# A block with timeline scheduling around the whole of a two-layer hybrid backbone

## The chip, the cores and the metric

The kernel runs on one core of one Trainium2 chip. The metric is device microseconds (us) of one execution. The core has five engines that take their instructions from queues of their own, in order: TensorE (PE, with its weight loads shown as PEld), VectorE (DVE), ScalarE (ACT), GpSimd (POOL) and SyncE (SP, which here only issues DMAs). An instruction that waits for a semaphore holds up all that stands behind it in the same queue. What stands where in these queues is fixed when the program is built.

## The reference

Two layers work on 1024 latent tokens and 256 context tokens of width 1024, all in float32:

```
for l in range(DEPTH):                      # 2
    mod = silu(c) @ w_mod[l] + b_mod[l]     # shift, scale, gate; also for c_ctx
    h  = rmsnorm(x,  g_pre[l]) * (1 + scale)   + shift
    hc = rmsnorm(xc, g_pre[l]) * (1 + scale_c) + shift_c
    u, uc = even_mixer(...) if l == 0 else odd_mixer(...)
    x = x + gate * rmsnorm(u @ w_out[l], g_post[l])
    if l == 0: xc = xc + gate_c * rmsnorm(uc @ w_out[l], g_post[l])

# even_mixer, per head (8 of them), m = 0, 1 two score maps
p[m] = softmax(rope(q[m]) @ rope(k[m]).T / 8)       # 1024+256 keys, 256 for context queries
o = rmsnorm((p[0] - lam * p[1]) @ v) * 0.8 * silu(g)
# beside it a gated short convolution over 1024 channels: b * conv3(c * h) * silu(g)
# odd_mixer: 16 heads of 2-D neighbourhood attention (NA), and
# 4 heads of gated linear attention (GLA) scanned in both directions
```

## The kernel before

One Python class, `Kernel`, writes the program. The methods are called one after the other, and each engine operation that they issue goes to a scheduler, which forms the five queues: among the operations that are ready in its own model of the machine it takes the one with the best priority. The priority is the place in the program, moved at some lines by offsets. So the queues don't follow the text of the program; the scheduler's model of how long things take decides what is put between what.

The weights come in units of 512 KB. `load_w` (L225) issues the DMA on SP, and `split_w` cuts the weight into a high part `whi` (ACT, L242) and a low part `wlo` (POOL or DVE, L243). `proj_chunk` (L438) multiplies one unit with one chunk of the tokens: 24 matmuls (8 steps of the contraction, times hi by hi, hi by lo and lo by hi) into a PSUM tile `pj`, of which there are two. A chunk has 512, 512 or 256 tokens.

Layer 0 runs eight heads of differential attention (`diff_head`). For each, k and q are projected and pass through `rope`: ACT copies the `pj` tile into an SBUF tile `ropex` (L517), which frees the `pj` tile, and DVE and POOL turn it. A head then has ten score blocks, each for two maps: `S` matmuls (L590), the row maximum on DVE (L592), the exponential on ACT (L594), DVE's combination of the two maps (L600), transposes on PE (`atr`, L612), their copies (L615, L616) and the products with v (`av`, L626). There is one `S` tile, so the next `S` matmuls wait until ACT has read the last. The head ends in `norm`: three `ms` matmuls (L636), then `rstd` with a Ln (L308) and an Exp (L309) on ACT and three passes on DVE (L310 to L312), the product with the gate (L638) and the DMA to DRAM (L639). Two buffers matter here:

```
big = self.ap.tile([P, 1280], F32, name="ropex", tag="p0", bufs=2)                                # in rope
r = self.rstd(ap.tile([P, TOK], F32, name="rs", tag="p0", bufs=2), ...)                           # in norm
```

`ropex`, the first map's probabilities and the norm's `rs` take turns in the same two buffers, `p0`. While `rs` holds one, from L309 to L638, the ropes have the other alone. Between the blocks the program calls `ws.run(1 + qt)`, which issues projection chunks of the convolution (`c4.0` and so on) and of w_mod as work that does not depend on the softmax.

The output projection `out0` (L754) follows; its three-bank pool takes the PSUM place of `S` and `ms`. Layer 1 has the GLA heads (gates `gz`, levels L1120 to L1162, key transposes `gktr` L1213, states and outputs L1233 and L1245) and the NA heads (scores L1464, L1465, products L1490, transposes L1513), and the second output projection.

At the start the program loads x, the sixteen early w_mod units and a small set of rows `rowsB` (L166), which PE transposes (`trB`, L169).

Of the kernel before, what the change touches and what calls it, by code (L numbers as in the profile page):

```python
# [39 lines left out]
class Stream:  # L40
# [39 lines left out]
    def run(self, n):  # L80
        for _ in range(n):
            if not self.step():
                return
# [15 lines left out]
class Kernel:  # L99
# [6 lines left out]
        return (ctx or self.ctx).enter_context(self.tc.tile_pool(name=name, bufs=bufs, **kw))  # L106

    def run(self):
        self.setup()
        with ExitStack() as es:  # L110
            self.hp = self.pool("hp", ctx=es)
            rope_es, out_es = ExitStack(), ExitStack()
            self.start(rope_es)
            conv_es = self.layer0(rope_es)
            self.layer1(self.out0(conv_es, out_es), out_es)
            with ExitStack() as es2:
                self.out1(es2)
# [1523 lines left out]
```

## Time and profile before

| | |
|---|---|
| median of 3 runs | 3095.2 us (3093.76 to 3097.55) |
| profiled execution | 3095.5 us, of which the span of the trace is 3093.7 us |
| PE busy | 2942.9 us, 95% of the span |
| PE weight loads busy | 2452.9 us, 79% |
| DVE, ACT, POOL busy | 1879.2, 1530.6 and 965.5 us |

PE's busy time is that of its matmuls from start to modelled end, and these overlap; a group of eight matmuls shows 1.98 us and the next group starts 1.82 us after it. The time that the profile lays down as idle before an instruction is time in which the engine had nothing running.

### The profile page before, as it was taken

What the parts mean: (1) busy time and instruction counts of PE and PEld (TensorE: products, weight loads), DVE (VectorE), ACT (ScalarE), POOL (GpSimd) and SP (SyncE); (2) the same over time, 40 slices, a digit from 0 to 9 for tenths busy, and PEclk for the clock granted to TensorE, in tenths of its full rate; (3) what the DMA queues carried; (4) which work ended last, traced back from release to release, by engine and by line L of the source; (5) the groups of instructions that cost most, each with busy time, mean ns of one, the idle gap of its engine ahead of it and who ended that gap; (6) DMA issues with size and microseconds to landing.
All of it is one profiled execution on the core that took longest, in us unless ns stands there. A gap on an engine that the chain in (4) does not pass through costs nothing. (4 is left out here: it accounts for less than half of the span.)

```text
span 3093.7 us, 42416 instructions
## 1 busy us (share of the span) xinstructions
PE 2942.9 (95%) x16244; PEld 2452.9 (79%) x16244; DVE 1879.2 (61%) x3149; ACT 1530.6 (49%) x2853; POOL 965.5 (31%) x765
## 2 busy tenths in 40 slices
PE   6999999999999999999999998999999999999898
PEld 4888888888888887888877777778777888887686
DVE  5675757575665757564244767575736666667723
ACT  4553535353544445453344665665635555556522
POOL 3213130313021211205233232322235555556622
PEclk9999999999999999999999999999999999999999
DMA  6111111211110211115342112111131111112323
GB/s 227 35 45 48 49 46 33 65 35 58 35 58 28 65 35 48 45 42 207 111 149 74 45 35 72 50 48 58 55 95 31 47 49 44 43 44 98 118 75 123
DMA packets 236982, 206.46 MB, mean 67 GB/s; under 512 B 43591, under 2 KB 194538, under 8 KB 236778
## 3 DMA queue, kind: packets, MB, share of 16 engines
q1 hardware_dynamic: 236778, 203.74, 21.4%
q8 instruction: 128, 2.10, 0.3%
q14 instruction: 76, 0.62, 0.1%
HBM read 168.04 MB, written 35.67 MB: 66 GB/s over the span
## 5 line engine op out<-in xcount | busy, mean ns | idle before, releaser
L243 POOL TENSOR_TENSOR wlo<-wraw,whi 128x1024 fp32r<-128x1024 f32 x149 | 371.6, 2494 | 1164.5 <-ACT whi L242 1014.9
L438 PE MATMUL pj<-hBh,whi 128*128 128x512 f32 (+1 forms) x1712 | 382.0, 353 | 9.7 <-ACT hBh L354 4.8
L438 PE MATMUL pj<-hBl,whi 128*128 128x512 f32 (+1 forms) x1712 | 370.3, 350 | 0.9 <-DVE hBl L355 0.9
L438 PE MATMUL pj<-hBh,wlo 128*128 128x512 f32 (+1 forms) x1712 | 350.7, 345 | 0.0
L242 ACT CAST whi<-wraw 128x1024 fp32r<-128x1024 f32 x176 | 184.5, 1048 | 308.7 <-PE ops L754 188.3
L438 PEld LDWEIGHTS pj<-hBh,whi 128*128 128x128 f32 x1712 | 275.3, 191 | 45.2 <-ACT hBh L354 5.4
L438 PEld LDWEIGHTS pj<-hBh,wlo 128*128 128x128 f32 x1712 | 278.7, 191 | 37.2
L438 PEld LDWEIGHTS pj<-hBl,whi 128*128 128x128 f32 x1712 | 279.5, 193 | 35.7 <-DVE hBl L355 1.1
L438 PE MATMUL pj<-hAh,whi 128*128 128x512 f32 x968 | 279.5, 409 | 14.6 <-ACT ropex L517 13.0
L438 PE MATMUL pj<-hAh,wlo 128*128 128x512 f32 x968 | 255.3, 398 | 0.0
L438 PE MATMUL pj<-hAl,whi 128*128 128x512 f32 x968 | 254.6, 394 | 0.0
L592 DVE TENSOR_REDUCE st<-S 128x1 f32<-128x1280 f32 (+1 forms) x160 | 203.8, 1274 | 79.3 <-PE S L590 79.3
L594 ACT ACTIVATE p<-S,st 128x1280 f32<-128x1280 f32 (+1 forms) x160 | 186.1, 1163 | 82.1 <-DVE st L592 80.5
L1472 POOL TENSOR_TENSOR np<-np,nst 128x640 f32<-128x640 f32 x128 | 166.6, 1304 | 192.3 <-DVE nst L1471 154.4
L438 PEld LDWEIGHTS pj<-hAh,wlo 128*128 128x128 f32 x968 | 181.0, 189 | 36.1
L438 PEld LDWEIGHTS pj<-hAh,whi 128*128 128x128 f32 x968 | 170.2, 191 | 47.9 <-ACT ropex L517 14.4
L438 PEld LDWEIGHTS pj<-hAl,whi 128*128 128x128 f32 x968 | 178.1, 189 | 34.7
L590 PE MATMUL S<-kst,qd 128*128 128x512 f32 (+1 forms) x832 | 192.3, 361 | 0.2 <-ACT p L594 0.2
L590 PEld LDWEIGHTS S<-kst,qd 128*128 128x128 f32 x832 | 137.1, 188 | 40.2 <-ACT p L594 21.5
L1468 DVE CUSTOM_DVE_ANT_0 np<-NS,nB 128x640 f32<-128x640 f32 x128 | 105.3, 823 | 90.4 <-PE NS L1465 84.5
L615 ACT CAST ath<-atr 128x512 fp32r<-128x512 f32 (+1 forms) x208 | 99.2, 505 | 113.5 <-PE atr L612 112.9
L1523 DVE TENSOR_TENSOR ptl<-ntr,pth 128x512 fp32r<-128x512 f32 (+2 forms) x224 | 117.5, 536 | 49.6 <-ACT pth L1522 45.7
(361 smaller groups left out, 6219.3 us busy)
## 6 DMA issues: line engine op xcount, KB each, us to landing
wraw<-in_ev_w_in_dram SPq DMA_DIRECT2D x64, 512.0 KB, 4.1
wraw<-in_od_w_in_dram SPq DMA_DIRECT2D x56, 512.0 KB, 3.9
wraw<-in_w_out_dram SPq DMA_DIRECT2D x55, 512.0 KB, 3.8
wraw<-in_w_mod_dram SPq DMA_DIRECT2D x48, 512.0 KB, 3.8
sgT<-gt SPq DMA_DIRECT2D x32, 256.0 KB, 2.0
uT<-sg SPq DMA_DIRECT2D x8, 640.0 KB, 3.5
nG<-in_rpbp_dram SPq DMA_DIRECT2D x128, 40.0 KB, 2.3
xt<-in_x_dram SPq DMA_DIRECT2D x8, 512.0 KB, 5.9
```

Source lines behind the costliest of these rows:

```text
L242: nc.scalar.copy(out=hi, in_=u.raw)
L243: (nc.vector if u.lo_eng == "v" else nc.gpsimd).tensor_tensor(out=lo, in0=u.raw, in1=hi.bitcast(F32), op=ALU.subtract)
L438: nc.tensor.matmul(ps[:, 0:tn], lhsT=a[:, k, :], rhs=self.h_at(k, t0, tn)[b], start=n == 0, stop=n == 23)
L590: nc.tensor.matmul(S[:, c0:c0 + tn], lhsT=qd[:, 2 * m + part, P * qt:P * qt + P], rhs=self.kst[m][:, t0:t0 + tn], start=part == 0, stop=pa ...
L592: nc.vector.tensor_reduce(out=st[:, m:m + 1], in_=S[:, 0:n], axis=AX.X, op=ALU.max, negate=True)
L594: nc.scalar.activation(out=p[m][:, 0:n], in_=S[:, 0:n], func=AF.Exp, bias=st[:, m:m + 1], accum_out=st[:, 2 + m:3 + m])
L615: nc.scalar.copy(out=dh, in_=tv)
L1468: nc.vector.tensor_tensor_reduce(out=p, in0=S[:, z0:z0 + 640], in1=bias[2 * i + m][:, c0:c0 + 640], scale=1.0, scalar=3e38, op0=ALU.add, o ...
L1472: nc.gpsimd.tensor_tensor(out=p, in0=p, in1=st[:, 2:3].broadcast_to([P, 640]), op=ALU.mult)
L1523: nc.vector.tensor_tensor(out=lv[:, s:e], in0=tr[:, s:e], in1=hv[:, s:e].bitcast(F32), op=ALU.subtract)
```

## The change

All of the program is put into one block of the tile framework, with a flag that makes the scheduler use another model of the machine (its timeline model) to decide the order. The computation, the number of instructions on every engine and the tiles stay as they are. The lines behind the new method stand four further down: L438 becomes L442, L590 becomes L594, L636 becomes L640.

```diff
     def run(self):
+        with self.tc.block(schedule_with_timeline_sim=True):
+            self.work()
+
+    def work(self):
         self.setup()
         with ExitStack() as es:
             self.hp = self.pool("hp", ctx=es)
```

The order of every queue is another. First place: PE at the end of the first head, from the last `ms` matmul on (`pj` are projection matmuls; `hA` and `hB` are the tokens, h high and l low). Before:

```order
L636 MATMUL ms<-qf,onesD 128x256
L438 MATMUL pj<-hAh,wlo 128x512 x8
L289 MATMUL modtr<-sel,modrow 128x2 x2
L438 MATMUL pj<-hBh,whi 128x512 x8
L438 MATMUL pj<-hBl,whi 128x512 x8
L438 MATMUL pj<-hBh,wlo 128x512 x8
L438 MATMUL pj<-hBh,whi 128x256 x8
L438 MATMUL pj<-hBl,whi 128x256 x8
L438 MATMUL pj<-hBh,wlo 128x256 x8
```

Of the change, at the same place:

```order
L640 MATMUL ms<-qf,onesD 128x256
L442 MATMUL pj<-hBh,whi 128x256 x8
L442 MATMUL pj<-hBl,whi 128x256 x8
L442 MATMUL pj<-hBh,wlo 128x256 x8
L442 MATMUL pj<-hAh,whi 128x512 x8
L442 MATMUL pj<-hAl,whi 128x512 x8
L442 MATMUL pj<-hAh,wlo 128x512 x8
```

In before, what follows `ms` are chunks of the convolution and, behind the rows shown, two more groups of 24 matmuls of 512 columns, before the first chunk whose `pj` tile a rope copy of the next head has to free. In the change, the next head's first two key chunks have been multiplied earlier, and the third, the 24 matmuls of 256 columns, follows `ms` directly: its tile is freed by the first rope copy (L521, in before L517), and the tile of the 24 matmuls behind it by the second. On ACT the queue there reads, of the change:

```order
L312 ACT_TABLE_LOAD
L312 ACTIVATE rt<-ms,eps 128x1280
L313 ACT_TABLE_LOAD
L313 ACTIVATE rs<-rt 128x1280
L521 COPY ropex<-pj 128x512
L246 CAST whi<-wraw 128x1024
L534 CAST ropex<-ropex 128x512
L521 COPY ropex<-pj 128x512
```

This is the order that before has at its seventh head's end and nowhere else; the change has it at the end of each of the first seven heads.

Second place: PE near the end of the first head, where the blocks of the last latent queries and of the context queries meet (`S` are scores, `kst` the keys, `atr` transposes, `av` products with v). Before:

```order
L590 MATMUL S<-kst_582,qd 128x512 x2
L590 MATMUL S<-kst_582,qd 128x256
L590 MATMUL S<-kst_582,qd 128x512 x2
L590 MATMUL S<-kst_582,qd 128x256
L438 MATMUL pj<-hBh,wlo 128x512 x7
L438 MATMUL pj<-hBh,whi 128x256 x8
L438 MATMUL pj<-hBl,whi 128x256 x5
L590 MATMUL S<-kst_583,qd 128x256 x2
L438 MATMUL pj<-hBl,whi 128x256 x3
L438 MATMUL pj<-hBh,wlo 128x256 x8
L270 MATMUL modps<-wraw,sst 32x256
L612 MATMUL atr<-ident,p_1752 128x128 x6
```

Of the change:

```order
L594 MATMUL S<-kst_583,qd 128x512 x2
L594 MATMUL S<-kst_583,qd 128x256
L594 MATMUL S<-kst_583,qd 128x512 x2
L594 MATMUL S<-kst_583,qd 128x256
L594 MATMUL S<-kst_584,qd 128x256 x2
L616 MATMUL atr<-ident,p_1753 128x128 x8
L594 MATMUL S<-kst_583,qd 128x256 x2
L630 MATMUL av<-ath,vh 128x256
L616 MATMUL atr<-ident,p_1753 128x128 x2
```

The projection matmuls that stood between the score groups have moved ahead of them. No projection follows until the head's end: the last score group, the `ms` matmuls and the last transposes stand next to each other too. The second to sixth heads read the same, the seventh has two such places, and the eighth has eight matmuls of 256 columns between the two score groups.

Third place: SP at the start (`xt` is x and ctx, `wraw` a weight unit of 512 KB). Before:

```order
L381 DMA xt<-in_x_dram 128x1024 x4
L225 DMA wraw<-in_w_mod_dram 128x4x256 x16
L381 DMA xt<-in_x_dram 128x1024 x2
L166 DMA rowsB<-in_ev_conv_dram 24x128
```

Of the change, behind the same four `xt`:

```order
L229 DMA wraw<-in_w_mod_dram 128x4x256 x9
L385 DMA xt<-in_x_dram 128x1024 x2
L229 DMA wraw<-in_ev_w_in_dram 128x8x128
L385 DMA xt<-in_x_dram 128x1024 x2
L229 DMA wraw<-in_ev_w_in_dram 128x8x128
L385 DMA xt<-in_ctx_dram 128x1024 x2
L229 DMA wraw<-in_w_mod_dram 128x4x256
L424 DMA cos<-in_cos_dram 128x1024
L425 DMA sin<-in_sin_dram 128x1024
L229 DMA wraw<-in_w_mod_dram 128x4x256
L229 DMA wraw<-in_ev_w_in_dram 128x8x128
L229 DMA wraw<-in_w_mod_dram 128x4x256 x5
```

Two more `wraw` of layer 0 follow, and then `rowsB`: eleven transfers of 512 KB (five weight units of layer 0, four `xt`, `cos` and `sin`) stand ahead of it that stood behind it. `trB` has kept its place in PE's queue.

## Rows read from the trace of the kernel before

**Rows 1.** The page, part 1: busy time and share of each engine.
```profile
PE 2942.9 (95%) x16244; PEld 2452.9 (79%) x16244; DVE 1879.2 (61%) x3149; ACT 1530.6 (49%) x2853; POOL 965.5 (31%) x765
```

**Rows 2.** Windows: stretch, length, busy PE, PEld, DVE, ACT, POOL; clock, DMA share, GB/s.
```profile
100.00:1200.00 1100.00, 1091.37 (x6263) 913.15 (x6262) 696.33 (x1110) 526.05 (x845) 216.76 (x114) 1.00 0.15 46
...
1700.00:2300.00 600.00, 548.61 (x3013) 460.04 (x3011) 400.41 (x560) 349.43 (x773) 167.87 (x135) 0.97 0.19 58
2300.00:2800.00 500.00, 482.19 (x2830) 410.45 (x2829) 326.54 (x694) 271.02 (x576) 272.14 (x291) 1.00 0.17 44
```

**Rows 3.** Waits of PE: line, releaser: us in total, times, longest.
```profile
PE gktr L1213 <- DVE KH L1189: 13.4, 8, 2.9
PE pj L438 <- ACT ropex L517: 13.0, 7, 5.3
PE NS L1464 <- DVE nqd L1453: 10.6, 8, 3.5
...
PE S L590 <- ACT p L594: 0.2, 1, 0.2
```

**Rows 4.** Timeline at the seventh head's end: start, us, engine, instruction [idle before].
```profile
1220.31 1.28 ACT L308 ACT_TABLE_LOAD   x1
...
1220.41 0.63 PE L636 MATMUL ms<-qf,onesD 128*128 128x256 f32 x2
...
1221.61 1.33 ACT L308 ACTIVATE rt<-ms,eps 128x1280 f32<-128x1280 f32 x1
...
1224.25 1.27 ACT L309 ACTIVATE rs<-rt 128x1280 f32<-128x1280 f32 x1
...
1225.04 1.99 PE L438 MATMUL pj<-hBl,whi 128*128 128x512 f32 x8
...
1225.43 0.57 ACT L517 COPY ropex<-pj 128x512 f32<-128x512 f32 x1
1225.56 1.49 DVE L310 SCALAR_TENSOR_TENSOR rt<-ms,rs 128x1280 f32<-128x1280 f32 x1 [2.12 <-ACT rs L309]
...
1226.86 1.98 PE L438 MATMUL pj<-hBh,wlo 128*128 128x512 f32 x8
...
1229.63 1.12 PE L438 MATMUL pj<-hBl,whi 128*128 128x256 f32 x8
...
1230.59 1.12 PE L438 MATMUL pj<-hBh,wlo 128*128 128x256 f32 x8
...
1234.83 1.48 DVE L638 TENSOR_TENSOR sg<-sg,rs 128x1280 f32<-128x1280 f32 x1
...
1236.35 0.59 ACT L517 COPY ropex<-pj 128x512 f32<-128x512 f32 x1 [0.78 <-DVE sg L638]
```

**Rows 5.** Timeline, a score block of 1280 keys and the next of 256, fourth head.
```profile
700.02 1.41 PE L590 MATMUL S<-kst,qd 128*128 128x512 f32 x6
...
701.46 1.49 DVE L592 TENSOR_REDUCE st<-S 128x1 f32<-128x1280 f32 x1 [0.81 <-PE S L590]
...
702.99 1.33 ACT L594 ACTIVATE p<-S,st 128x1280 f32<-128x1280 f32 x1 [1.20 <-DVE st L592]
...
704.46 0.50 PE L590 MATMUL S<-kst,qd 128*128 128x256 f32 x2
...
704.63 1.55 DVE L600 SCALAR_TENSOR_TENSOR p<-p,st,p 128x1280 f32<-128x1280 f32 x1
```

**Rows 6.** Timeline, the last score block of the seventh head and its norm.
```profile
1215.17 0.45 PE L590 MATMUL S<-kst,qd 128*128 128x256 f32 x2
...
1216.82 1.04 PE L636 MATMUL ms<-qf,onesD 128*128 128x512 f32 x2
```

**Rows 7.** Timeline of PE behind the wait of rows 4.
```profile
1236.99 3.78 PE L438 MATMUL pj<-hAh,whi 128*128 128x512 f32 x8 [5.28 <-ACT ropex L517]
```

**Rows 8.** Window at the start, columns as in rows 2.
```profile
15.00:30.00 15.00, 12.61 (x84) 7.47 (x84) 4.39 (x15) 2.01 (x3) 1.29 (x1) 1.00 1.10 348
```

**Rows 9.** Timeline of PE at the start.
```profile
38.27 0.22 PE L169 MATMUL trB<-ident,rowsB 35*128 35x35 f32 x1 [1.81 <-DMA rowsB<-in_od_gate_bias_dram]
```

## Prediction, before the result

> **What bounds the kernel now.** I read the page first, for the share of each engine. PE is busy for 2942.9 us [rows 1], so it has 3093.7 - 2942.9 = 150.8 us without work in the whole span. No other engine comes near. The windows come next, to see where the 150.8 us lie. From 100 to 1200 us, which is layer 0 but for its last head, PE is busy for 1091.37 of 1100 us: 8.6 us idle. From 1700 to 2800 us, the GLA and NA heads, it is idle for 51.4 + 17.8 = 69 us [rows 2]. So layer 0 is bound by PE's work, and layer 1 by PE's work and some short waits. Third, the list of what PE waits for names them: key products, score operands, and, from layer 0, seven waits for the rope copy with 13.0 us in all, of which one has 5.3. The score matmuls of layer 0 waited for their exponential once, 0.2 us [rows 3]. Last, the timeline at that one long wait, since it shows what a head's end costs when PE has little else to do.
>
> **What the change can do.** It adds and removes no operation, so PE's work stays. What changes is which work lies between an operation and the one that waits for its result. The sum is therefore made of idle time of PE, place by place, and a stall of PE in layer 0 is paid in full, since almost no idle time is left there that could absorb it.
>
> **Head ends, +78 us.** At the seventh head's end the trace has the very order on ACT and DVE that the change has at all seven. The last `ms` matmuls end at 1220.41 + 0.63 = 1221.04. Behind them ACT runs two table loads, the Ln and the Exp, and then the first rope copy, which ends at 1226.0. DVE's passes follow, the product L638 ends at 1236.3, and only then is the buffer free that the second rope copy takes; that copy ends at 1236.94 [rows 4]. From `ms` to there are 15.9 us. Eight matmuls of 512 columns take 1226.86 - 1225.04 = 1.82 us, eight of 256 columns 0.96 us [rows 4]. Before had 32 and 24 of them in the 15.9 us, some 10.6 us with a small transpose of w_mod, and waited for the rest, 5.3 us; the first six heads had more work than the wait is long. The change has the 24 of 256 columns, 2.9 us, and they too must wait for the first copy. So 15.9 - 2.9 = 13.0 us idle, seven times, 91 us. Off it goes what the rope waits cost now, 13.0 us [rows 3]. For a lower bound, a head's end that costs only what the seventh costs today would give 7 x 5.3 - 13.0 = +24; the upper bound is the chain without any cover, 7 x 15.9 - 13.0 = +98. I take 78, as the quoted order leaves nothing else to run.
>
> **Score groups without cover, +60 us.** In the middle of a head, an `S` group of 1280 keys is followed by its maximum, its exponential and the next group, 704.46 - 700.02 = 4.44 us from start to start [rows 5]. Its six matmuls are 1.15 us of PE's time at the rates above, so 3.3 us must be covered by projections. Today they are; in the change that place has none. The transposes behind wait for L600, which ends at 706.18 [rows 5]: 706.18 - 704.46 less 0.24 for two matmuls is 1.5 us. The last group and `ms` are 1.65 us apart [rows 6], 1.4 us without cover. Two smaller steps after it, the last transposes and the square ahead of the last `ms`, I put at 1.0 us together: three projection matmuls (0.7 us) lie in the second today. That is 3.3 + 1.5 + 1.4 + 1.0 = 7.2 us in each of six heads, 43 us. The seventh has a second such place, in part covered by ten transposes and two projection matmuls: 10.5 us. The eighth keeps 0.96 us of cover: 6.2 us. Together 60. A wait for the gate's activations, which stand on ACT among these, could come on top; bounds are 40 (only the 1280-key step, 3.3 eight times, and the last one, 1.4 eight times) and 75.
>
> **End of layer 0, +6 us.** The change goes from the eighth head's last `ms` straight to out0, whose PSUM is that of `ms` and free when L310 has read it: from 1221.04 to 1225.56 + 1.49 = 1227.05 in the same chain [rows 4], 6.0 us. Before has 122 projection matmuls of 512 and 256 columns there. Bounds 0 and 16, the second if the whole chain counts.
>
> **PE's clock, +25 us.** Behind the 5.28 us wait eight matmuls took 3.78 us [rows 7] where eight take 1.98 [rows 4]: the granted clock was at the lower of its two levels, 1.2 GHz, after PE had stood still. So a stall of this kind costs 1.8 us more. There are seven head ends and eight uncovered score groups of 3.3 us, and one such place is paid already: 14 x 1.8 = 25. Bounds 11 (head ends alone, less that one) and 45. The Trainium skill ("TensorE: Matmul & The Clock Gate", Part 1) says that the slow state is the default and that activity releases it; the 3.78 us agree. Without that effect the sum would be 25 us less.
>
> **Start, +8 us.** Eleven transfers of 512 KB now come ahead of `rowsB`. At 348 GB/s [rows 8] that is 11 x 0.524 / 0.348 = 16.6 us, and `trB`, which waited 1.81 us and ran at 38.27 [rows 9], runs near 55. What is fetched ahead is needed just after, and PE's work behind `trB` is short, so I take half; bounds -4 and +20.
>
> **Layer 1, -10 us.** The order there puts more between a product and its reader at most places (the gates of a group are issued well ahead), and less at a few. The most it could bring is all of the idle time, 69 us, and the slow clock that goes with it, 0.03 of 600 us, 18 us [rows 2]: -87. The loss at its worst is another +20. I take -10, since the waits of rows 3 are each about 1.5 us and come from short chains that have to run in any order.
>
> **Sum.** 78 + 60 + 6 + 25 + 8 - 10 = +167 us on the profiled execution's 3095.5 us (its span and 1.8 us around it), which is 0.3 us from the median: 3262 us, 5.4% slower.
>
> **Rivals.**
> 1. Layer 1 gives back all it can, -87 in place of -10: 3185 us. For it speaks that PE's waits there are for DVE and POOL chains of a few operations, which is what a better order hides; against it that such a chain is serial from one chunk to the next, and has to run in any order. Chance 0.17.
> 2. Faster: the stalls of layer 0 are not paid. This would be so if PE had slack that lets it catch up behind each head's end. Its weight loads are busy for 79% only [rows 1], and 913 of 1100 us in layer 0 [rows 2]; if the missing 17% were room, a loss of 20 us a head would be made good within the head. Then layer 1's -87 and the start's +8 remain: 3016 us. It decides from the point where a head loses under 79 / 8 = 10 us. Against it: eight matmuls of 512 columns follow each other at 1.82 us and no queue ahead of them is empty, so the pace is that of the columns, and a stall stays. The Trainium skill ("Perfetto Trace Analysis", Identifying the Most-Contended Engine) tells one to judge TensorE's room by the busy share of the weight loads and not by that of the matmuls; by it 79% would mean room. The trace does not bear that out here, as the 1.82 us pace holds through stretches in which PE never waits. Chance 0.06.
> 3. Heavier: no term of layer 0 has any cover and the start costs its +20: 98 + 75 + 16 + 45 + 20 + 20 = +274, 3370 us. Chance 0.05.
> 4. Nothing happens. The rows of the order exclude that the queues are the same; it would need gains and losses that cancel. Chance 0.02.
>
> The forecast itself has 0.70. Its own spread is the terms' near bounds: 3215 to 3320. The range reaches down to the first rival, and a little below: 3165 to 3320, which leaves out rivals 2 to 4, 0.13. Faster by over 0.2% (about what a measurement of this kernel can tell from no change) is rival 2, 0.06; within 0.2% is rival 4, 0.02; the rest, 0.92, is slower.
>
> **What would show it.** In the profile of the changed kernel, PE's wait for the rope copy (now L521) should have the largest total, near 90 us in seven pairs of waits; the waits of `S` (L594) and `ms` for the exponential, 0.2 us today, should come to 30 us or more; busy PE from 100 to 1200 us should fall from 1091 to about 970, with a granted clock near 0.96; `trB` should run near 55 us; out0 should start with a wait of 6 us for DVE. I am wrong if the head ends show short waits, which would mean that their queues run apart from each other by more than I read from the order, or if layer 1's idle time all but goes.

## The result, and the profile after

The changed kernel takes 3412.7 us (median of 3 runs, 3410.5 to 3418.2) against 3095.2: a ratio of 1.1028, 95% interval 1.1003 to 1.1053, 10% slower. That is the predicted direction, but nearly twice the predicted loss, and above the range. The profiled span is 3408.7 us, 315.0 more than before.

The page of the changed kernel, part 1, is the row that answers to [rows 1]:

```profile
PE 3026.0 (89%) x16244; PEld 2560.5 (75%) x16244; DVE 1887.7 (55%) x3149; ACT 1522.3 (45%) x2853; POOL 959.2 (28%) x765
```

PE has the same 16244 matmuls and is busy for 83.1 us more with them; its idle time rose from 150.8 to 3408.7 - 3026.0 = 382.7, by 231.9. The two make the 315.0. The mean granted clock of the execution fell from 0.987 to 0.939. What PE waits for, from the list of PE's waits (us in total, times, longest), the answer to [rows 3]:

```profile
PE pj L442 <- ACT ropex L521: 78.6, 14, 6.6
PE S L594 <- ACT p L598: 32.5, 18, 3.0
PE NS L1468 <- DVE nst L1472: 23.2, 28, 2.1
PE modps L274 <- DMA wraw<-in_w_mod_dram: 20.9, 9, 8.8
PE pj L442 <- DVE csg L218: 17.4, 12, 2.6
PE gl L1124 <- DVE KQ L1157: 16.2, 11, 1.9
PE ops L758 <- ACT uh L743: 16.1, 1, 16.1
...
PE atr L616 <- DVE p L604: 10.4, 8, 1.4
...
PE ms L640 <- ACT p L598: 9.0, 8, 1.2
...
PE ms L640 <- ACT qf L633: 3.8, 8, 0.5
```

Where before had three kinds of wait of more than 10 us in total, the changed kernel has twelve. (The nine waits of `modps`, 20.9 us against 8.3 before, all lie in the first 52 us, at the start.) The next views say in which stage the time went. The first matmul of out0 starts at 1644.1 us (before 1404.3), the first GLA gate at 1923.4 (1693.8), the first NA score at 2610.9 (2322.9), and the last NA product at 3241.2 (2921.3):

| stage | before, us | after, us | difference |
|---|---|---|---|
| start and layer 0, to the first `ops` matmul | 1404.3 | 1644.1 | +239.8 |
| out0 | 289.5 | 279.3 | -10.2 |
| GLA heads | 629.1 | 687.5 | +58.4 |
| NA heads | 598.4 | 630.3 | +31.9 |
| rest | 172.4 | 167.5 | -4.9 |

Windows of before for one head, from the first head's last `ms` to the second's, and for the GLA and NA stages (columns as in [rows 2]):

```profile
221.00:387.50 166.50, 165.09 (x947) 138.09 (x946) 104.85 (x168) 78.77 (x128) 34.31 (x18) 1.00 0.16 47
...
1693.80:2322.90 629.10, 575.95 (x3150) 482.55 (x3148) 406.15 (x569) 361.38 (x793) 175.89 (x142) 0.98 0.19 56
2322.90:2921.30 598.40, 568.12 (x3343) 482.17 (x3344) 418.02 (x869) 341.84 (x724) 342.60 (x353) 0.99 0.19 53
```

The same of the changed kernel, with the stretch of [rows 2] first:

```profile
100.00:1200.00 1100.00, 984.84 (x5425) 838.47 (x5425) 621.09 (x943) 442.16 (x717) 197.28 (x105) 0.94 0.14 41
274.00:467.00 193.00, 172.52 (x947) 147.00 (x946) 109.48 (x170) 78.10 (x128) 34.25 (x18) 0.94 0.13 40
...
1923.40:2610.90 687.50, 606.17 (x3168) 515.89 (x3168) 393.72 (x570) 361.58 (x794) 168.34 (x146) 0.92 0.18 53
2610.90:3241.20 630.30, 566.02 (x3326) 491.86 (x3325) 414.46 (x869) 340.99 (x724) 343.81 (x350) 0.98 0.19 51
```

One head has the same 947 matmuls. It takes 26.5 us more: idle time goes from 1.4 to 20.5, and the matmuls themselves take 7.4 us longer, as the granted clock falls from 1.00 to 0.94. The GLA stage pays in the same two coins: idle from 53 to 81 us (+28), busy +30 at a clock of 0.92 for 0.98 (some 4 of the 30 are 19 more projection matmuls that now stand there). NA pays in idle time alone, 30 to 64 us.

The timeline of the changed kernel shows the places (start, duration, engine, instruction, idle before it): the start, a gate wait, the score groups, the second head's end, layer 0's end, a GLA chain, the way into the NA heads and an NA wait.

```profile
55.08 0.29 PE L173 MATMUL trB<-ident,rowsB 35*128 35x35 f32 x1 [2.63 <-DMA rowsB<-in_ev_conv_dram]
...
420.60 1.88 PE L442 MATMUL pj<-hBh,whi 128*128 128x256 f32 x8 [2.60 <-DVE csg L218]
...
451.11 0.50 PE L594 MATMUL S<-kst,qd 128*128 128x256 f32 x2 [3.03 <-ACT p L598]
...
452.89 1.97 PE L616 MATMUL atr<-ident,p 128*128 128x128 f32 x8 [1.28 <-DVE p L604]
...
466.89 0.70 PE L640 MATMUL ms<-qf,onesD 128*128 128x256 f32 x2 [0.47 <-ACT qf L633]
...
471.97 0.57 ACT L521 COPY ropex<-pj 128x512 f32<-128x512 f32 x1
...
472.59 2.07 PE L442 MATMUL pj<-hBh,whi 128*128 128x256 f32 x8 [5.00 <-ACT ropex L521]
...
474.46 1.56 PE L442 MATMUL pj<-hBl,whi 128*128 128x256 f32 x8
...
481.38 1.48 DVE L642 TENSOR_TENSOR sg<-sg,rs 128x1280 f32<-128x1280 f32 x1
...
482.90 0.59 ACT L521 COPY ropex<-pj 128x512 f32<-128x512 f32 x1 [0.78 <-DVE sg L642]
...
483.54 3.78 PE L442 MATMUL pj<-hAh,whi 128*128 128x512 f32 x8 [6.56 <-ACT ropex L521]
487.12 2.94 PE L442 MATMUL pj<-hAl,whi 128*128 128x512 f32 x8
489.89 2.00 PE L442 MATMUL pj<-hAh,wlo 128*128 128x512 f32 x8
...
1627.28 0.70 PE L640 MATMUL ms<-qf,onesD 128*128 128x256 f32 x2 [0.47 <-ACT qf L633]
...
1638.57 0.32 SPq L643 DMA_DIRECT2D uT<-sg  x1
1638.98 4.96 SPq L742 DMA_DIRECT2D ul<-uT  x8
...
1643.17 0.83 ACT L743 CAST uh<-ul 128x768 fp32r<-128x768 f32 x1 [10.73 <-DMA ul<-uT]
...
1644.06 0.79 PE L758 MATMUL ops<-whi,uh 128*128 128x512 f32 x1 [16.08 <-ACT uh L743]
...
2020.71 1.13 PE L1124 MATMUL gl<-KQ 128*128 128x128 f32 x8 [1.50 <-ACT KQ L1155]
2023.59 1.13 PE L1124 MATMUL gl<-KQ 128*128 128x128 f32 x8 [1.75 <-ACT KQ L1155]
2026.47 2.04 PE L1124 MATMUL gl<-KQ 128*128 128x128 f32 x8 [1.75 <-DVE KQ L1157]
...
2573.30 2.05 PE L442 MATMUL pj<-hBh,whi 128*128 128x256 f32 x8 [9.22 <-DVE nk L1382]
...
2812.61 0.46 PE L1468 MATMUL NS<-nk,nqd 128*128 128x384 f32 x1 [1.53 <-DVE nst L1472]
```

At the head's end the chain is that of [rows 4]: `ms`, two tables, Ln, Exp, the first rope copy at 471.97, DVE's passes, the product L642 that frees the `rs` buffer, the second copy at 482.90. From the end of `ms` to 483.54 it lasts 16 us, and PE has 24 matmuls of 256 columns in it. Behind each wait PE is slow for a while: the first eight matmuls of 256 columns take 1.87 us from start to start and not 0.96, and the two groups of 512 columns behind the second wait take 3.58 and 2.77 us and not 1.82, together 2.7 us more.

### The profile page after: what moved, and what is told of

Its sections match the earlier page's. It is cut to its first block, busy times and chain, and to the rows that moved or that the text cites. A ratio compares the mean times of both kernels' runs of the same rounds, so it can differ in the third digit from the quotient of the medians.

```text
span 3408.7 us, 42483 instructions
## 1 busy us (share of the span) xinstructions
PE 3026.0 (89%) x16244; PEld 2560.5 (75%) x16244; DVE 1887.7 (55%) x3149; ACT 1522.3 (45%) x2853; POOL 959.2 (28%) x765
## 5 line engine op out<-in xcount | busy, mean ns | idle before, releaser
L247 POOL TENSOR_TENSOR wlo<-wraw,whi 128x1024 fp32r<-128x1024 f32 x149 | 381.9, 2564 | 1075.9 <-ACT whi L246 859.7
L442 PE MATMUL pj<-hBh,whi 128*128 128x512 f32 (+1 forms) x1712 | 376.8, 361 | 68.0 <-ACT ropex L521 35.0
L442 PEld LDWEIGHTS pj<-hBh,whi 128*128 128x128 f32 x1712 | 291.8, 200 | 118.5 <-ACT ropex L521 37.8
L442 PE MATMUL pj<-hBh,wlo 128*128 128x512 f32 (+1 forms) x1712 | 376.8, 350 | 0.0
L442 PE MATMUL pj<-hBl,whi 128*128 128x512 f32 (+1 forms) x1712 | 369.9, 356 | 2.4 <-DVE hBl L359 2.4
L442 PE MATMUL pj<-hAh,whi 128*128 128x512 f32 x968 | 275.1, 424 | 53.4 <-ACT ropex L521 43.6
L442 PEld LDWEIGHTS pj<-hBl,whi 128*128 128x128 f32 x1712 | 290.2, 201 | 39.1 <-DVE hBl L359 2.6
L442 PEld LDWEIGHTS pj<-hBh,wlo 128*128 128x128 f32 x1712 | 278.4, 193 | 33.1
L442 PEld LDWEIGHTS pj<-hAh,whi 128*128 128x128 f32 x968 | 187.2, 204 | 97.3 <-ACT ropex L521 45.0
L442 PE MATMUL pj<-hAh,wlo 128*128 128x512 f32 x968 | 259.4, 395 | 0.0
L442 PE MATMUL pj<-hAl,whi 128*128 128x512 f32 x968 | 253.1, 400 | 0.0
L594 PE MATMUL S<-kst,qd 128*128 128x512 f32 (+1 forms) x832 | 196.2, 367 | 37.1 <-ACT p L598 32.5
L442 PEld LDWEIGHTS pj<-hAl,whi 128*128 128x128 f32 x968 | 187.0, 195 | 39.4
L442 PEld LDWEIGHTS pj<-hAh,wlo 128*128 128x128 f32 x968 | 175.4, 188 | 33.4
L594 PEld LDWEIGHTS S<-kst,qd 128*128 128x128 f32 x832 | 145.5, 197 | 63.3 <-ACT p L598 38.1
L620 DVE TENSOR_TENSOR atl<-atr,ath 128x512 fp32r<-128x512 f32 (+1 forms) x208 | 118.0, 584 | 129.9 <-ACT ath L619 128.5
L525 POOL TENSOR_TENSOR ropex<-ropex,sin 128x512 f32<-128x512 f32 x32 | 57.7, 1803 | 422.8 <-DVE ropex L523 422.8
```

The costliest lines, as they stand in the source:

```text
L247: (nc.vector if u.lo_eng == "v" else nc.gpsimd).tensor_tensor(out=lo, in0=u.raw, in1=hi.bitcast(F32), op=ALU.subtract)
L442: nc.tensor.matmul(ps[:, 0:tn], lhsT=a[:, k, :], rhs=self.h_at(k, t0, tn)[b], start=n == 0, stop=n == 23)
L525: nc.gpsimd.tensor_tensor(out=s, in0=s, in1=self.sin[:, t0:t0 + tn], op=ALU.mult)
L594: nc.tensor.matmul(S[:, c0:c0 + tn], lhsT=qd[:, 2 * m + part, P * qt:P * qt + P], rhs=self.kst[m][:, t0:t0 + tn], start=part == 0, stop=pa ...
L620: nc.vector.tensor_tensor(out=atl[:, g0:g0 + gn, P * qt:P * qt + P], in0=tv, in1=dh.bitcast(F32), op=ALU.subtract)
```

## The experiments

Ratios are to the kernel before, taken on the same chip. In the diffs a minus line is of the kernel that is edited. The diffs show only the lines that matter; `...` stands for what is left out within a line.

**One part alone.** The same block was put around the start and layer 0 only, without the flag (e1) and with it (e2); around the start only, with it (e7) and without (e8); and the first part without the flag, with the flag on the context, meant to leave layer 1 under it (e3).

```diff
+            with self.tc.block():                # e2: block(schedule_with_timeline_sim=True)
                 self.start(rope_es)
                 conv_es = self.layer0(rope_es)
+            u = self.out0(conv_es, out_es)
+            self.layer1(u, out_es)
```

> The start and layer 0 stand in a block of their own without the flag; the rest follows outside it, also without the flag. The order of each engine's queue is that of the kernel before, but that nothing crosses the end of layer 0. Theory A (only the order of the queues matters): 3095 to 3105 us. Rival B (a block itself costs, by its entry and exit): tens of us more, 3130 or above.

> As the split without the flag, but the block of start and layer 0 has the flag. Out0, layer 1 and out1 are in the default order. Theory A (the loss lies in the order, stage by stage, and the stages add up): the changed kernel's first ops matmul came 240 us later than in before, of which 16 were the wait of out0 that the default order of the rest would cover, so +220 to +240, 3315 to 3335 us. Rival C (the loss of layer 1 follows from layer 0, by clock or by late weights): 3380 us or more.

> The other way round: start and layer 0 in a block without the flag, all that follows with it. Theory A: the stages behind the first ops matmul took 75 us more in the changed kernel (out0 -10, GLA +58, NA +32, out1 -5), so 3165 to 3175 us. Rival C: 3095 to 3110 us, since layer 0 is undisturbed.

e1 took 3111.3 us (1.0047, 1.0032 to 1.0062), above what theory A allowed: the cut costs 15 us, of which one wait of 12.2 us at layer 0's end is most. e2 took 3336.2 (1.0775, 1.0758 to 1.0791). Its rope waits come to 78.1 us in 14, as in the changed kernel, and from the first GLA gate on it takes 1402 us where e1 takes 1399. So under the flag the start and layer 0 lose 225 us and leave nothing to layer 1; the other 76 of 3412.7 - 3336.2 belong to what layer 1's own order does. e3 took 3414.3 (1.1026, 1.1009 to 1.1042), and its head ends stand in the changed kernel's order: the flag on the context acts inside the plain block too. It is the changed kernel with a cut and says nothing on layer 1 alone, which was not run by itself.

> Only the start (conditioning, x, the first token chunks) stands in a block with the flag; all heads and the rest are in the default order. Against the next run, which has the same cut without the flag. Theory A: the start is where about 20 of the 53 us lie by which the first head ended later in the changed kernel (21 of these are work done ahead, some 12 the uncovered waits in the head): 15 to 25 us above the next run. My forecast had 8.

> The start in a block of its own without the flag. The cut at its end costs something, as nothing crosses it: 3095 to 3115 us.

e7: 3112.9 (1.0053, 1.0040 to 1.0067). e8: 3106.0 (1.0032, 1.0020 to 1.0044). The flag at the start costs 6.8 us and not the 15 to 25 that the expectation had. In e7 `modps` waits as it does in the changed kernel (21.0 us), so these waits are part of the 6.8.

**The buffer of the head's end.** In the changed kernel `rs` got a buffer that no rope copy uses (e4); the same edit was made in the kernel before (e5).

```diff
-            r = self.rstd(ap.tile([P, TOK], F32, name="rs", tag="p0", bufs=2), ...)
+            r = self.rstd(self.ap2.tile([P, 10, 256], F32, name="rs", tag="ath").rearrange(...)[:, 0:TOK], ...)
```

> The changed kernel, with the norm's tile rs in the buffer of ath (free at a head's end) in place of one of the two that the ropes use. The second rope copy then doesn't wait for the product L642. Theory A1 (the head ends' chain is what layer 0 loses most by): by 13.0 us of idle and 2.7 us of slow clock in seven places, -110 us, 3300 us. Rival D (the work that covers is only so much, and cover at the head's end is taken from another place in the head): -30 us or less, 3380 us or more.

> The kernel before with rs in the buffer of ath. TensorE's order is the same row by row; only the second rope copy no longer waits for L638 at the seventh head's end, the one place where before has the changed kernel's order. Theory A1: the 5.3 us wait goes, with the 1.8 us of slow clock behind it: 3087 to 3090 us. Rival (the wait moves to the next operation): 3094 to 3097 us.

e4: 3288.2 (1.0623, 1.0605 to 1.0641), 124 us less than the changed kernel. The first of PE's waits in e4:

```profile
PE S L594 <- ACT p L598: 43.6, 19, 3.9
```

The rope copy is gone from the list, and 11 us of the gain come back as score waits. e5: 3095.6 against 3096.0 (0.9998, 0.9990 to 1.0007). There the long wait of [rows 7] is gone, and a new one stands behind a later rope copy, as the timeline of e5 shows:

```profile
1247.57 1.68 ACT L579 CAST qd<-qf 64x256 fp32r<-64x256 f32 x4 [5.66 <-POOL qf L541]
...
1249.93 3.78 PE L438 MATMUL pj<-hAh,whi 128*128 128x512 f32 x8 [4.13 <-ACT ropex L517]
```

On ACT that copy stands behind the casts of q, which wait for POOL. So the buffer is what stretches the head's end in the changed kernel; in the kernel before, which has one such end, the wait moved to the next chain and nothing was won.

**Work that depends on nothing, put into the head's end.** In the changed kernel each head got sixteen matmuls behind its norm whose result is not used (e6).

```diff
+            extra = self.ps_av.tile([P, 512], F32, name="extra", tag="av")
+            for _ in range(16):
+                nc.tensor.matmul(extra, lhsT=self.onesD, rhs=self.qf[:, 768:1280], start=True, stop=True)
```

> The changed kernel with 16 more matmuls of 512 columns right behind the last ms matmuls of each head (their result is not used). At some 0.45 us each, the pace of the ms matmuls, that is 7.2 us a head, 58 us of PE's work in all. Theory A (PE stands idle there for 13 us a head): they fall into the wait and keep the clock up, 3390 to 3415 us. Rival E (PE's work is what counts, and a wait at one place is made good at another): 3412 + 58 = 3470 us.

e6: 3405.2 (1.0999, 1.0984 to 1.1014), 7.5 us less than without them. The two intervals overlap, so what this shows is that the added work costs nothing, not that it gains. The extra matmuls are larger than the expectation says, since each matmul stands as two in the trace. From the timeline of e6:

```profile
467.14 13.99 PE L646 MATMUL extra<-qf,onesD 128*128 128x512 f32 x32
480.56 1.51 PE L442 MATMUL pj<-hBh,whi 128*128 128x256 f32 x8
...
483.83 2.00 PE L442 MATMUL pj<-hAh,whi 128*128 128x512 f32 x8
```

The chunk that waits for the second rope copy starts at 483.83, in the changed kernel at 483.54, and now at full speed: eight matmuls in 2.00 us, not 3.78. Windows over the eight heads, of e6 and then of the changed kernel, say where 8 x 14 = 112 us of work went:

```profile
200.00:1630.00 1430.00, 1341.41 (x7206) 1096.85 (x7204) 819.50 (x1258) 594.15 (x967) 256.86 (x138) 0.97 0.15 45
```
```profile
200.00:1630.00 1430.00, 1265.52 (x6952) 1075.36 (x6950) 821.87 (x1252) 591.63 (x965) 265.90 (x138) 0.93 0.15 43
```

Busy PE rises by 75.9 us and not by 112; the other 36 come from the matmuls that are there anyway, in a stretch whose granted clock is 0.97 instead of 0.93. What fails at the head's end is therefore not PE's pace but the lack of independent work.

**How early the projections are spent.** In the kernel before, without the flag, `ws.run` issues its chunks earlier in the head and so leaves fewer for the end (e17, e18).

```diff
-            ws.run(1 + qt if qp < 4 else 0)
+            ws.run(2 if qp < 4 else 0)           # e18: 2 + qt
```

> The kernel before, no flag, with two projection steps behind each of the first eight score blocks (before: one and two in turn), so that less is left for the head's end. Behind the last ms matmuls of heads one to six the order has 34 matmuls of 512 columns ahead of the first that waits for the second rope copy, beside the 24 of 256 columns; at the seventh 2. By the 15.9 us chain: 15.9 - 7.7 - 2.9 = 5.3 us idle and 1.8 of slow clock six times, 12.5 and 2.7 at the seventh where before has 5.3 and 1.8, less six waits of 1.3 that go: +43, 3138 us. Rival H (it needs the flag: the default order keeps its cover in the heads and loses nothing): 3093 to 3105 us.

> The same with two and three steps in turn. The order has 12 matmuls of 512 columns there and none at the seventh: 15.9 - 2.7 - 2.9 = 10.3 us idle and 2.7 of slow clock six times, 13.0 and 2.7 at the seventh, less the same: +79, 3174 us. Rival H: 3093 to 3105 us.

e17: 3147.1 (1.0172, 1.0155 to 1.0189); e18: 3200.2 (1.0343, 1.0327 to 1.0358). Timeline of e17, then of e18, one head's end each, and e18's waits:

```profile
422.07 3.79 PE L438 MATMUL pj<-hAh,whi 128*128 128x512 f32 x8 [5.35 <-ACT ropex L517]
```
```profile
425.76 1.22 PE L438 MATMUL pj<-hBh,whi 128*128 128x256 f32 x8 [2.25 <-ACT ropex L517]
...
436.71 3.78 PE L438 MATMUL pj<-hAh,whi 128*128 128x512 f32 x8 [6.31 <-ACT ropex L517]
```
```profile
PE pj L438 <- ACT ropex L517: 64.6, 14, 7.8
PE ops L754 <- ACT uh L739: 18.2, 1, 18.2
```

With the same scheduler as before, the more is spent early, the longer the same wait gets: 5.4 us at this head's end in e17, 2.3 + 6.3 = 8.6 in e18, where before has one wait of 1.3 us and the changed kernel 11.6 in two. The flag is not needed for a loss of this kind; an order that uses up the projections early is enough, and in e18 it costs 106 of the 225 us that layer 0 loses under the flag. Both came out above the sums (3138 and 3174), e17 by 9 and e18 by 26 us. The sums left out the end of layer 0, 10.5 and 18.2 us of wait, which is all of it in e17. In e18 transposes wait too, 12.4 us for L600, and the rope waits are 10 us less than the 74.8 of its sum.

**The tail of the head.** On top of e4, two chunks were kept for the last two blocks (e9); the same edits in the kernel before (e10).

```diff
-            ws.run(1 + qt if qp < 4 else 0)
+            ws.run((1, 1, 1, 1, 1, 1, 1, 1, 2, 2)[n])
```

> The run with rs in the buffer of ath (3288 us), and the program hands out its twelve projection steps of a head as one behind each of the first eight score blocks and two behind each of the last two, in place of one and two in turn behind the first eight. In the order, 23 projection matmuls of 512 columns stand between the last score group and the ms matmuls, and projections follow within ms. Theory A2 (score groups without projections between them are what is left in layer 0): the waits of S, atr and ms, 72 us in that run with their slow clock, fall by two thirds: 3225 to 3250 us. Rival D (cover put in one place is missing in another): 3275 us or more.

> The same two edits on the kernel before, without the flag. In before nothing in the heads waits but at the seventh head's end, so there is nothing to win there: 3090 to 3105 us by both theories; faster than 3090 only if the steps behind the last blocks also cover the seventh head's rope.

e9: 3308.4 (1.0683, 1.0669 to 1.0698), 20 us slower than e4. e10: 3096.8 against 3096.5 (0.9999, 0.9990 to 1.0008). From e9's waits of PE:

```profile
PE S L594 <- ACT p L598: 30.8, 17, 3.0
...
PE pj L442 <- DVE csg L218: 19.6, 13, 2.6
```

The score waits fall by 13 us as meant, and the wait for the gate's product rises from 7.7 to 19.6, with others behind it. The first theory is wrong here: chunks moved in the text only move the place without cover.

**Offsets.** The three priority offsets of layer 1 were taken out under the flag (e11) and without it (e12): `with self.tc.high_priority(offset=...)` becomes `with ExitStack()`.

> The changed kernel with its three priority offsets (-6 for the level operands, 60 for the NA queries, -20 for the NA copies) taken out. All three act in layer 1 alone. Rival F (layer 1 loses since offsets that suit one machine model mislead the other): layer 1 gets its 76 us back in good part, 3350 to 3390 us. Theory A (the model spends the projections early, with or without offsets): within 20 us of 3412.

> The kernel before without the same three offsets: what they are worth in the default order. 3095 to 3150 us; the run above is read against it.

e11: 3397.5 (1.0969, 1.0954 to 1.0984), 15 us less than the changed kernel; e12: 3106.0 (1.0031, 1.0019 to 1.0043), 9.5 more than before. That the offsets mislead the other model is a third of layer 1's loss at most: 15, or 25 with what they bring without the flag, of 76. The GLA stage has it: 667.5 us in e11 for 687.5.

**Pacing.** A one-column DVE copy into the `pj` tile, from a value that a later block makes, holds each projection chunk back until that block has begun: in the heads of layer 0 (e13), in layer 1 (e14), in both (e15), and in both in the kernel before (e16).

```diff
+        if self.hold is not None:
+            nc.vector.tensor_copy(ps[:, 0:1], self.hold)
```

> The changed kernel with the projections of a head paced: before a chunk's first matmul DVE copies one column of the next score block's first row maximum into its PSUM tile (overwritten at once), so that the chunk can't be scheduled earlier. The flag stays. The order then has 1 to 6 us of projections between most score groups and 5 to 8 us at the head's end, where it had 2 to 8 and nothing. Theory A3 (the flag's order spends 5 to 8 us of projections on score steps that need 3.3, and has none left for the end): the rope wait at the head ends falls under 15 us in all, and of the 205 us that the heads lose some 130 come back, 3270 to 3300 us. Rival D (the projections don't suffice for this order, wherever they stand): 3390 us or more.

> The same pacing in layer 1 alone: a chunk waits for the level's column of R in the GLA heads, and for the next block's row minimum in the NA heads. In the order no NA gap has over 6 us of projections any more (98 us of them stood in such gaps, 41 in before); in the GLA heads 196 us stand in gaps over 6 us, in place of 250 (155 in before). Theory A3: NA's 32 us come back for the most part, of GLA's 58 little, 3370 to 3390 us. Rival G (layer 1 loses by its chains on DVE and POOL, whose order changed too): 3405 us or more.

> Both pacings together. If the stages add up, the gains of the two runs above add up: 3230 to 3270 us by theory A3.

> Both pacings in the kernel before, without the flag: what the copies and the dependence themselves cost where the order was even already. In the order the projections between score groups become less even (0 and 5 us in turn, where they had 2 to 4). Theory A3: slower than before by the uncovered groups, 3130 to 3250 us.

e13: 3488.1 (1.1273, 1.1254 to 1.1292); e14: 3403.0 (1.0993, 1.0976 to 1.1011); e15: 3477.8 (1.1239, 1.1221 to 1.1258); e16: 3342.1 (1.0804, 1.0787 to 1.0822). From e13's waits of PE:

```profile
PE S L597 <- ACT p L601: 84.2, 34, 5.1
PE pj L445 <- ACT ropex L524: 50.2, 8, 6.6
PE atr L620 <- DVE atl L624: 49.7, 44, 2.1
```

The rope waits fall by 28 us and the score and transpose waits rise by far more. The hold by itself costs 248 us in the kernel before, some 100 of them in layer 1, so none of e13 to e15 can say what a good spread under the flag would be worth. e14 is 10 us below the changed kernel with intervals that overlap, nearer to the rival's price than to the theory's: the GLA stage takes 673.0 us for 687.5 and NA 637.6 for 630.3, and the `NS` wait for `nst` keeps its 23 us.

None of the versions beats the kernel before.

## Why the prediction was right in direction and too low

Of the 148 us between the forecast's 167 and the 315.0 of the span, layer 1 is 85 (+75 where -10 was forecast) and the clock in layer 0 is 36 (61 where 25 was forecast). The gate wait without a price is 17, the end of layer 0 is 10 and some 16 are smaller waits; head ends and score groups came out 17 lower. With layer 1 as forecast the time would be some 3327 us, still above the range's 3320, so two steps failed: layer 1 and the price of the clock.

Of the signs that the prediction named, the rope waits, those of `S` and `ms` (41.5 us), busy PE from 100 to 1200 us (984.8 for 970), its clock (0.94 for 0.96) and `trB` came; out0's wait did not come as described. Neither sign of being wrong came, since both looked for a smaller loss.

**Head ends (+78), right.** +65.6: the rope waits went from 13.0 to 78.6 us, seven pairs of waits with 11.6 us in the pair shown, where the sum had 13.0; the order and the chain are those read from [rows 4]. e6 and e18 show the cause: it is missing work, not a slower chain. That `rs` holds the buffer is what stretches it (e4).

**Score groups without cover (+60), right.** `S` 32.5, `atr` 10.4, `ms` 9.0 and 3.8: 55.7 us, against 0.2 in before, with 3.03 us for the 1280-key step (3.3 predicted). The wait for the gate's activations, which the prediction named and gave no price, is 17.4 us more: `csg` in the list.

**Start (+8), right:** 6.8 by e7 and e8, and `trB` at 55.08.

**End of layer 0 (+6), too small:** 16.1, its upper bound, though for another reason. I let out0 wait for its PSUM. It waits for data: on SP's queue the store of the last head's `uT` (L643), which needs L642, stands ahead of the loads of `ul` (L742), so the whole norm chain and a DMA lie on the path.

**PE's clock (+25), wrong in size, beyond its bound of 45:** 61. PE's busy time rose by 83.1 us with the same matmuls, 61 of it ahead of out0 with the same 7812 matmuls (7.4 in the one head shown); the 30 in the GLA stage belong to layer 1 below. I counted one price of 1.8 us for each head's end and each score group. A head's end has two waits with 1.3 us (0.9 and, by its 1.56 for 1.12, 0.4) and 2.7 us of it behind them. Short waits can be followed by slow matmuls too: the eight transposes at 452.89, behind waits of 3.03 and 1.28 us, take 1.97 us. Of the three `gl` groups from 2020.71 on, each behind a wait of 1.50 or 1.75 us, the first two take 1.13 and the third 2.04, at a granted clock of 0.50, the lower level. The Trainium skill ("TensorE: Matmul & The Clock Gate", Part 1) has the slow state as the default that activity lifts; the trace agrees, with 0.50 behind these waits, and e6, which fills waits and gets 36 us of other work's time back, shows it from the other side.

**Layer 1 (-10, at worst +20), wrong: about +75.** This is the larger of the two steps that failed. I read from the order that more stands between a product and its reader at most places, and held the short serial chains to cost the same in any order. In the trace PE's idle time rises by 28 us in GLA and by 34 in NA, and GLA's clock falls. The total of projection work there is nearly the same, but it lies in clumps: of 54 groups of `gl` matmuls 25 are followed by the next with no projection matmul between, in before 3 of 60; of NA's 136 score groups 74 are, in before 43 of 135. Stretches of over 6 us of projections hold 251 of the 299 us between the `gl` groups, in before 155 of 294. The `gl` rows from 2020.71 on show such a bare chain.

Most of the new idle time stands in the bare places. In NA they hold 49.5 of 64 us, in before 7.6 of 30; in GLA 22.4 of 81, in before nothing. One more is the way into the NA heads, where the first key projections wait 9.2 us (2573.30), in before 3.8. What I should have counted was places with nothing between, as I did in layer 0, not places with more. But their number alone gives no price either: a bare place of NA costs 0.7 us here and cost 0.2 in before.

That this loss is layer 1's own and not layer 0's delay is shown by e2. That the bare places cause it is read from the profile alone: e14 left no stretch of over 6 us in NA, but also 74 bare places of 130, and NA's idle time stayed at 63 us; e11 leaves the offsets a third at most.

**The rivals.** Layer 1 gave nothing back (rival 1). The faster case (rival 2) took the idle part of the weight loads for room. The Trainium skill ("Perfetto Trace Analysis", Identifying the Most-Contended Engine) reads TensorE's room from its share of the peak FLOP rate and the busy share of the weight loads; by the second alone 79% would have left some. The trace does not bear that out: the share fell to 75% while the time rose by 10%. No head caught up: each of heads 2 to 6 loses 26 to 28 us. e6 says where room is: in the waits, 112 us of work for nothing. The heavier case (rival 3, 3370) was nearer than my forecast, for another reason than the one given: layer 1 and the clock, not the start.

**What stays open:** why the other machine model forms these clumps, and what of layer 1's 75 us the bare places cause; no run takes them away, and the flag was not run on layer 1 by itself.

## What to carry to other kernels

Where one engine is busy for 99% of a stage, an order can only lose there: count, at each serial chain (a norm, a softmax, a scan), the independent work that stands in it before and after, and price every place that goes bare; a total or a mean of cover says nothing, since surplus at one place doesn't pay for lack at another. Look at the queue that issues loads as well: a load behind a store that waits for the chain's end puts the whole chain on the path. And before believing a price of idle time, add the clock's part from the busy time of the same instructions.

## What the runs showed of the hardware that was not expected

The same 16244 matmuls took 83 us longer, with the mean granted clock at 0.939 for 0.987, in an order that makes PE wait more often. In the GLA stage, where most waits are under 3 us long, the granted clock was 0.92 and some 26 of 606 us came from it. And 112 us of matmuls with no use, placed in the waits, did not make the kernel slower, since the matmuls behind them ran at full speed.
